# A one-core hybrid decoder step: VectorE takes the state-space block's products with C and its decay, and all sums of squares

## The chip, the cores and the metric

The kernel runs on one core of a Trainium2 chip. The metric is the device time of one execution in microseconds (us); lower is better. The engines named in the text are TensorE (PE, with its weight loads PEld), VectorE (DVE), ScalarE (ACT), GpSimd (POOL) and the DMA-issuing queue SP. Each engine works through its own instructions in the order in which they stand in the program.

## The reference

One layer over 1032 columns (1024 prompt positions and 8 sample positions), all in float32:

```
proj = rmsnorm(x) @ w_in                     # z | xBC | dt | v
xbc  = silu(causal_dwconv(xBC)); xs, B, C = split(xbc)
# state-space block, 24 heads of 64, chunks of 128 positions, state 64
acum = cumsum(dt * a)                        # within a chunk
mix  = (C B^T) * exp(acum_l - acum_s) * dt   # l >= s
y    = mix @ xs + (C * exp(acum)) @ h        # h: the state that enters the chunk
h    = exp(acum_last) * h + chunk_states     # the state that leaves it
y    = grouped_rmsnorm((y + d_skip * xs) * silu(z))
x    = x + [y | pooling(v)] @ w_out
u    = causal_dwconv(rmsnorm(x) @ w_up)
x    = x + (silu(gate(u)) * value(u)) @ w_down
out  = rmsnorm(x)
```

The states after the step are outputs too.

## The kernel before

Channels lie on partitions and positions along the free dimension. Every large product is made of three products of float32r parts: a weight tile is split into a high part (ACT, L140) and a low part (L141, on DVE or POOL; both stand in `weight_parts`), an activation tile likewise (L210, L211 in `split`), and the matmuls are L159 to L161, L1120 or L1307. The tile framework orders the instructions of each engine from a simulated timeline, so a change of an engine can move its neighbours; semaphores carry the waits.

**Input projection with the state-space block (`ssd_phase`).** Tiles of w_in go through PE one after another (`conv_tile`, `gate_tile`), three pieces of 344 columns each (24 matmuls a piece, 72 a tile). The three additions of the causal convolution are DVE's L516. Between the pieces stand the steps of the state-space block: two halves (q = 0 beside the convolution tiles, q = 1 beside the gate tiles), each with 8 chunks. Chunk c goes through

- `decay`: the exponent differences (DVE L538), 12 exponentials on ACT (L188, tile `mix`), and for c > 0 the tile `ce`: an exponential of 128x768 on ACT and its product with C (tile from `self.ctl`), L553 on POOL;
- `turn`: transposes on PE (L565, L571, L574), copies and products on DVE (L575, L576, L578 into `xd`, L583 into `mix`);
- `apply`: on PE the new chunk state (L597 into `pM`) and the output (L620 with `mix`, L630 with `ce` and the old state `h`, into `pY`). The state that goes on is h * decay (L606, POOL), to which DVE adds the chunk state (L610). DVE's L638 adds D times x.

`sample_tile` (L660 to L682) does one step for the 8 sample positions, all on POOL; tiles 0 to 2 come after half q = 0, tiles 3 to 6 inside half q = 1, each held behind the latest L606 (`self.pl`). `gate_tile` multiplies with silu(z) (L698, L700), and after three tiles `group_norm` squares on ACT (L712) and adds the squares up (L714, on POOL for the first two groups, on DVE for the others).

**End of w_out (`w_out_end`).** Two halves of 516 columns, 8 tiles n each. PE makes 24 matmuls of 258 columns a tile, DVE adds them to the residual x (L971), ACT squares the tile (L978), POOL adds the squares of n = 1 to 5 into `ssq` (L983); the last two squares and `ssq` go through a product with ones (L986, L997), which ACT turns into `rn` (L188). Beside the second half runs work on the first one (`beside`): scaling by `rn` in DVE's L1004 and splitting (L210, L211) into the operands of the up-projection.

**Up- and down-projection.** L1120 is fed by combined weights, made by DMAs that add (L1098 on SP loads, L1100 on POOL adds). The down-projection squares its output tiles on ACT (L1370, L1373) and adds the squares up on POOL (L1374).

Of the kernel before, what the change touches and what calls it, by code (L numbers as in the profile page):

```python
# [13 lines left out]
ALU = mybir.AluOpType  # L14
# [4 lines left out]
P = 128  # L19
# [26 lines left out]
TH, TQ = 516, 258  # L46
# [29 lines left out]
class Kernel:  # L76
    def __init__(self, ctx, tc, d):
        self.ctx, self.tc, self.nc, self.d = ctx, tc, tc.nc, d
        nc = self.nc
        pool = lambda name, bufs=1, **kw: ctx.enter_context(tc.tile_pool(name=name, bufs=bufs, **kw))  # L80
        self.const = pool("const")
        self.wpool = pool("weights")
        self.big = pool("big", 30)
        self.dram = pool("scratch", 1, space=DRAM)

        self.cst = self.const.tile([P, NCONST], F32, name="cst")
        self.mat = self.const.tile([P, NMAT], F32, name="mat")
        self.conv_st = self.const.tile([P, 16, 35], F32, name="conv_st")
        self.ones = self.const.tile([P, P], F32, name="ones")
        nc.vector.memset(self.ones, 1.0)  # L90
        self.zero = self.const.tile([P, P], mybir.dt.bfloat16, name="zero")
        nc.vector.memset(self.zero, 0.0)
        self.eps = self.const.tile([P, 1], F32, name="eps")
        nc.gpsimd.memset(self.eps, EPS)
        self.ident = self.mat[:, M_ID : M_ID + P]
        self.uid = 0
        self.lo_eng = nc.vector
        self.hooks = []
        self.pl = None
        self.tab = self.set = None  # L100
        self.table_set(EXPLN)

# [426 lines left out]
    def decay(self, q, c):  # L529

        nc = self.nc
        h0 = 12 * q
        mix = self.ph.tile([P, 12, P], F32, tag="mix", name=self.nm("mix"), bufs=2)
        src = lambda h, n, p: self.acd[c : c + 1, h * P : (h + n) * P].partition_broadcast(p)
        nc.sync.dma_start(mix.rearrange("p r l -> p (r l)"), src(h0, 12, P))
        hs = c * NH + h0

        nc.vector.scalar_tensor_tensor(  # L538
            out=mix, in0=self.acl[:, hs : hs + 12].unsqueeze(2).broadcast_to([P, 12, P]), scalar=80.0, in1=mix,
            op0=ALU.subtract, op1=ALU.max,  # L540
        )
        ce = None
        if c > 0:
            ce = self.ph.tile([P, 6, P], F32, tag="ce", name=self.nm("ce"), bufs=2)
            for g in range(2):
                rows = slice(64 * g, 64 * g + 64)
                nc.sync.dma_start(ce[rows].rearrange("p r l -> p (r l)"), src(h0 + 6 * g, 6, 64))
        for r in range(12):
            self.tables(mix[:, r], mix[:, r], AF.Exp, bias=self.acl[:, hs + r : hs + r + 1], scale=-1.0)
        if c > 0:  # L550
            self.tables(ce, ce, AF.Exp, scale=-1.0)
            cc = self.ctl[q][:, c * P : (c + 1) * P]
            nc.gpsimd.tensor_tensor(out=ce, in0=ce, in1=cc.unsqueeze(1).broadcast_to([P, 6, P]), op=ALU.mult)  # L553
        return mix, ce

    def turn(self, q, c, mix):
# [31 lines left out]
    def apply(self, q, c, mix, ce, xd, bT):  # L588

        nc = self.nc  # L590
# [11 lines left out]
        if c == 0:  # L602
            nc.scalar.activation(h1, pst[:, :384], AF.Copy)
        else:
            by_head = lambda t: t.rearrange("p (r x) -> p r x", x=64)
            self.pl = nc.gpsimd.tensor_tensor(  # L606
                out=by_head(h1), in0=by_head(h),
                in1=self.cd[:, c, q].unsqueeze(2).broadcast_to([P, 6, 64]), op=ALU.mult,
            ).ins
            nc.vector.tensor_tensor(out=h1, in0=h1, in1=pst[:, :384], op=ALU.add)  # L610
        self.hst[q] = h1
        if c == NCH - 1:
# [21 lines left out]
        for g in range(2):  # L634
            for i in range(3):
                k = 6 * q + 3 * g + i
                t = self.xs[k][:, cols]
# [69 lines left out]
    def group_norm(self, g):  # L707
        nc = self.nc
        sq = [self.short(SW, "sq") for _ in range(2)]
        nc.scalar.activation(sq[0], self.xs[3 * g], AF.Square)  # L710
        for i in range(1, 3):
            nc.scalar.activation(sq[1], self.xs[3 * g + i], AF.Square)  # L712
            eng = nc.gpsimd if g < 2 else nc.vector
            eng.tensor_tensor(out=sq[0], in0=sq[0], in1=sq[1], op=ALU.add)  # L714
        self.later(2, lambda: self.group_scale(g, sq))

    def group_scale(self, g, sq):
# [36 lines left out]
    def ssd_phase(self):  # L754
# [39 lines left out]
                queue.append(lambda c=c: step(c))  # L794

        def sample(i):
            with self.behind(self.pl):
                self.sample_tile(i // 6, i)

        self.lo_eng = nc.gpsimd  # L800
        for n in range(1, 6):
# [92 lines left out]
    def w_out(self, pf):  # L894
# [51 lines left out]
        def beside(n):  # L946
            if n == 0:
                return
            for k in {1: (0, 1), 2: (2, 3), 5: (4, 5), 6: (6, 7)}.get(n, ()):
                self.scale(k, 0)  # L950
            for k in {3: (0, 1), 4: (2, 3), 6: (4, 5), 7: (6, 7)}.get(n, ()):
                t = self.op_tile()
                self.split(self.x2[k][:, :TH], t[:, 0], t[:, 1])
                self.ops["p1" if k < half else "p2"].append((t[:, 0], t[:, 1]))
# [3 lines left out]
    def w_out_end(self, ops, t, beside=None):  # L958
# [5 lines left out]
        for n in range(KT):  # L964
# [13 lines left out]
                act = nc.scalar.activation(sq, x[:, cols], AF.Square).ins  # L978
            with self.behind(act):
                nc.scalar.dma_start(self.x2d[n][:, cols], x[:, cols])  # L980
            if n > 0:
                if n < 6:
                    nc.gpsimd.tensor_tensor(out=ssq, in0=ssq, in1=sq, op=ALU.add)  # L983
                else:
                    for q in range(2):
                        nc.tensor.matmul(  # L986
                            pb[q][:, :TQ], self.ones, sq[:, q * TQ : (q + 1) * TQ], start=(n == 6), stop=False
                        )
# [323 lines left out]
    def down(self, ops):  # L1312
# [49 lines left out]
        mksq = lambda: self.ph.tile([P, TH], F32, tag="sq", name=self.nm("sq"), bufs=2)  # L1362
        ssq = [self.bigt(F32, TOK, "ssq") for _ in range(2)]
        begun = set()

        def square(n, t):

            if t not in begun:
                begun.add(t)
                nc.scalar.activation(ssq[t][:, :TH], x2[n][:, half(t)], AF.Square)  # L1370
            else:
                sq = mksq()
                nc.scalar.activation(sq, x2[n][:, half(t)], AF.Square)  # L1373
                nc.gpsimd.tensor_tensor(out=ssq[t][:, :TH], in0=ssq[t][:, :TH], in1=sq, op=ALU.add)  # L1374

        def r_of(t):
            return ssq[t][:, TH : 2 * TH]
# [1 line left out]
        for p in DOWN[:-1]:  # L1379
# [17 lines left out]
            for m in range(NM):  # L1397
                ps = [self.gps() for _ in range(2)]
                for s in range(NS):
                    both = self.down_weights(p, m, s)  # L1400
                    for q in range(2):
                        self.piece(ps[q][:, :TQ], both, ops, s, q)
                for q in range(2):
                    sink(p, m, q, ps[q][:, :TQ])
                if p == "p6":
                    square(2 * m, 0)
                elif p == "p4":
                    square(2 * m + 1, 0)
                    square(2 * m + 1, 1)
        p = DOWN[-1]  # L1410
        ops = self.down_ops(p)
        both = {}
# [207 lines left out]
```

## Time and profile before

| | |
|---|---|
| median of 3 runs | 1403.05 us (1397.98, 1403.52, 1403.05) |
| the profiled execution's own time | 1399.9 us |
| its span, first to last instruction | 1398.1 us |
| mean granted TensorE clock | 0.984 |
| PE idle from 0 to 57 us, 142 to 238 us, 275 to 400 us, 682 to 735 us, 1160 us to the end | 4.0, 4.1, 11.9, 8.5, 9.9 us |

The stretch from 142 to 238 us holds half q = 0 of the state-space block, 275 to 400 us most of half q = 1, 682 to 735 us the end of w_out and the start of the up-projection, 735 to 1160 us the rest of the up-projection. The granted clock is the share of full speed that TensorE was given. In the rows of the profile, "out<-in" names tiles, and in brackets or after a bar stands how long the engine had been idle before and who ended that.

### The profile page before, as it was taken

To read this page: it belongs to the slowest core of one execution; us is meant where nothing else is said; L and a number is where in the kernel's file an instruction comes from. 1 tells how busy PE (TensorE), PEld (TensorE's weight loads), DVE (VectorE), ACT (ScalarE), POOL (GpSimd) and SP (SyncE) were. 2 spreads that over 40 slices of the span, in tenths; PEclk is the share of its full clock that TensorE was granted. 3 is DMA by queue.
4 is the path that set the end of the run, shared out by engine and by line. 5 is a ranking of instruction groups with operands and counts; after the bars stand their busy time and mean duration, and the time that the engine had idled before them with its cause. 6 is when DMAs were issued, how large, how long until landed. Compare 5 with 4: busy or idle time off the path is not lost.

```text
span 1398.1 us, 26823 instructions
## 1 busy us (share of the span) xinstructions
PE 1359.6 (97%) x10360; PEld 1312.8 (94%) x10360; DVE 986.9 (71%) x1501; ACT 701.3 (50%) x1408; POOL 496.8 (36%) x656
## 2 busy tenths in 40 slices
PE   8999999988999999999979999999999999999997
PEld 7799879977799999999979999999999999999997
DVE  6575899588864685755789867776776787567743
ACT  6346774655645451312447545554555465444451
POOL 4233466888578202122321222221222223214122
PEclk9999999999999999999989999999999999999999
DMA  7031235252331258665586877777777869657513
GB/s 250 1 109 39 87 121 173 81 162 98 95 105 63 73 187 280 224 199 187 151 199 151 210 202 197 199 191 200 176 179 199 204 214 324 225 180 238 179 54 121
DMA packets 117819, 228.08 MB, mean 163 GB/s; under 512 B 19884, under 2 KB 37116, under 8 KB 117692
## 3 DMA queue, kind: packets, MB, share of 16 engines
q1 hardware_dynamic: 73772, 130.21, 29.7%
q0 software_dynamic: 27056, 70.22, 20.0%
q10 hardware_dynamic: 16864, 25.95, 5.6%
q8 instruction: 81, 1.33, 0.4%
q14 instruction: 46, 0.38, 0.1%
HBM read 169.64 MB, written 45.15 MB: 154 GB/s over the span
## 4 chain that ended last, share of the span: by engine, by line
PE 82%; DVE 7%; DMA 3%; POOL 3%; issue 3%; ACT 2%; DVEq 0%; SPq 0%; POOLq 0%; ACTq 0%
PE g L1120 30%; PE g L1307 15%; PE g L160 10%; PE g L161 10%; PE g L159 10%; DVE wop L141 1%; DVE mix L583 1%; PE pY L620 1%; DVE xd L578 1%; POOL st L680 1%; DMA s<-wup 1%; DVE xs L516 1%; DVE xs L638 1%; PE pY L630 1%; DVE mix L538 1%
## 5 line engine op out<-in xcount | busy, mean ns | idle before, releaser
L1120 PE MATMUL g<-op,wop 128*128 128x258 f32 x3696 | 448.0, 284 | 3.9 <-ACT op L1045 3.7
L1120 PEld LDWEIGHTS g<-op,wop 128*128 128x128 f32 x3696 | 446.9, 190 | 4.7 <-ACT op L1045 4.1
L140 ACT ACTIVATE wop<-raw 128x512 fp32r<-128x512 f32 (+1 forms) x208 | 125.9, 608 | 228.1 <-PE g L161 134.3
L1307 PE MATMUL g<-op,wop 128*128 128x258 f32 x1848 | 224.9, 283 | 1.6 <-ACT op L210 0.8
L159 PE MATMUL g<-hh,wop 128*128 128x344 f32 x696 | 226.3, 325 | 0.0
L160 PE MATMUL g<-hl,wop 128*128 128x344 f32 x696 | 225.6, 324 | 0.0
L161 PE MATMUL g<-hh,wop 128*128 128x344 f32 x696 | 225.1, 323 | 0.0
L1307 PEld LDWEIGHTS g<-op,wop 128*128 128x128 f32 x1848 | 222.5, 189 | 2.6 <-ACT op L210 1.0
L141 DVE TENSOR_TENSOR wop<-raw,wop 128x512 fp32r<-128x512 f32 (+1 forms) x186 | 139.2, 752 | 88.6 <-ACT wop L140 86.6
L140 ACT ACTIVATE wop<-s 128x512 fp32r<-128x512 f32 (+1 forms) x136 | 83.6, 620 | 140.2 <-PE g L1307 51.9
L159 PEld LDWEIGHTS g<-hh,wop 128*128 128x128 f32 x696 | 132.5, 190 | 1.2 <-issue 1.1
L161 PEld LDWEIGHTS g<-hh,wop 128*128 128x128 f32 x696 | 132.3, 190 | 1.2 <-issue 1.2
L160 PEld LDWEIGHTS g<-hl,wop 128*128 128x128 f32 x696 | 132.2, 190 | 0.5 <-issue 0.4
L1100 POOL DMA_DIRECT2D s<-s x44 | 37.7, 857 | 249.8 <-DMA s<-wup 114.4
L1202 DVE SCALAR_TENSOR_TENSOR acc<-u,cst,acc 128x1048 f32<-128x1048 f32 x88 | 115.2, 1309 | 12.2 <-ACT acc L1200 10.6
L141 DVE TENSOR_TENSOR wop<-s,wop 128x512 fp32r<-128x512 f32 (+1 forms) x136 | 92.2, 683 | 36.3 <-ACT wop L140 33.9
L1180 DVE TENSOR_TENSOR u<-u,g 128x258 f32<-128x258 f32 (+2 forms) x176 | 58.2, 355 | 71.5 <-PE g L1120 64.1
L1177 ACT ACTIVATE u<-g 128x258 f32<-128x258 f32 (+2 forms) x220 | 69.6, 340 | 70.2 <-PE g L1120 70.0
L161 PE MATMUL g<-yh,wop 128*128 128x344 f32 x288 | 92.0, 319 | 0.0
L160 PE MATMUL g<-yl,wop 128*128 128x344 f32 x288 | 91.9, 320 | 0.0
L159 PE MATMUL g<-yh,wop 128*128 128x344 f32 x288 | 91.8, 319 | 0.0
L1277 POOL DMA_DIRECT2D g<-td x77 | 41.1, 539 | 122.9 <-DVE op L211 69.4
(276 smaller groups left out, 2279.8 us busy)
## 6 DMA issues: line engine op xcount, KB each, us to landing
s<-wup SPq DMA_DIRECT2D x88, 256.0 KB, 3.1
g<-td POOLq DMA_DIRECT2D x77, 258.0 KB, 4.6
raw<-wup SPq DMA_DIRECT2D x66, 256.0 KB, 3.9
raw<-win SPq DMA_DIRECT2D x58, 256.0 KB, 2.6
mix<-acd SPq DMA_DIRECT2D x16, 768.0 KB, 4.5
td<-acc ACTq DMA_DIRECT2D x22, 516.0 KB, 6.2
s<-wup POOLq DMA_DIRECT2D x44, 256.0 KB, 5.4
s<-s POOLq DMA_DIRECT2D x44, 256.0 KB, 3.7
```

The costliest lines, as they stand in the source:

```text
L140: self.nc.scalar.activation(hi, raw[:, :w], AF.Copy)
L141: lo_eng.tensor_tensor(out=lo, in0=raw[:, :w], in1=hi.bitcast(F32), op=ALU.subtract)
L159: nc.tensor.matmul(ps[:, :n], wh, xh[:, sl], start=(first and k == 0), stop=False)
L160: nc.tensor.matmul(ps[:, :n], wh, xl[:, sl], start=False, stop=False)
L161: nc.tensor.matmul(ps[:, :n], wl, xh[:, sl], start=False, stop=(final and k == last))
L1100: nc.gpsimd.dma_start(t, raw[acc] if acc in raw else w[acc][j], accum_op=ALU.add)
L1120: nc.tensor.matmul(out, a, b, start=(p in OPENS and j == 1), stop=(j == 12), skip_group_check=True)
L1177: a = nc.scalar.activation(out, ps[:, s], AF.Copy, scale=-1.0 if p in ("p5", "p4") else 1.0)
L1180: nc.vector.tensor_tensor(out=out, in0=out, in1=ps[:, s], op=op)
L1202: nc.vector.scalar_tensor_tensor(out=acc, in0=u[:, k : k + FW], scalar=self.c("fw", 3 * n + k), in1=acc, op0=ALU.mult, op1=ALU.add)
L1277: self.loaded = self.nc.gpsimd.dma_start(st[:, j], self.td[i + j][ROW[p]]).ins
L1307: self.pe = nc.tensor.matmul(out, a, b, start=(s == 0 and i == 0 and j == 0), stop=(s == len(PIECES) - 1 and i == nk - 1 and j == 2),).ins
```

## The change

Four places lose their POOL instruction and gain the same one on DVE: the product of `ce` with C, the decay of the state, the squares of the first two norm groups, and the squares at the end of w_out and of the down-projection. The last two are now added one tile late: `w_out_end` adds the square of tile n - 1 behind the last addition of tile n, and the down-projection empties a list `waiting` at its next square. `sample_tile` is no longer held behind the decay. In `beside`, the scaling of tiles 6 and 7 and the splitting of tiles 4 and 5 move from n = 6 to n = 7, behind the last addition of w_out.

```
 decay():
-            nc.gpsimd.tensor_tensor(out=ce, in0=ce, in1=cc...broadcast_to([P, 6, P]), op=ALU.mult)
+            nc.vector.tensor_tensor(out=ce, in0=ce, in1=cc...broadcast_to([P, 6, P]), op=ALU.mult)
 apply():
-            self.pl = nc.gpsimd.tensor_tensor(
+            nc.vector.tensor_tensor(
                 out=by_head(h1), in0=by_head(h),
                 in1=self.cd[:, c, q].unsqueeze(2).broadcast_to([P, 6, 64]), op=ALU.mult,
-            ).ins
+            )
 group_norm():
-            eng = nc.gpsimd if g < 2 else nc.vector
-            eng.tensor_tensor(out=sq[0], in0=sq[0], in1=sq[1], op=ALU.add)
+            nc.vector.tensor_tensor(out=sq[0], in0=sq[0], in1=sq[1], op=ALU.add)
 ssd_phase():
-            with self.behind(self.pl):
-                self.sample_tile(i // 6, i)
+            self.sample_tile(i // 6, i)
 w_out():
-            for k in {1: (0, 1), 2: (2, 3), 5: (4, 5), 6: (6, 7)}.get(n, ()):
+            for k in {1: (0, 1), 2: (2, 3), 5: (4, 5), 7: (6, 7)}.get(n, ()):
                 self.scale(k, 0)
-            for k in {3: (0, 1), 4: (2, 3), 6: (4, 5), 7: (6, 7)}.get(n, ()):
+            for k in {3: (0, 1), 4: (2, 3), 7: (4, 5, 6, 7)}.get(n, ()):
 w_out_end():
+            if 1 < n < 7:
+                with self.behind(add):
+                    nc.vector.tensor_tensor(out=ssq, in0=ssq, in1=before, op=ALU.add)
             if n > 0:
-                if n < 6:
-                    nc.gpsimd.tensor_tensor(out=ssq, in0=ssq, in1=sq, op=ALU.add)
-                else:
+                before = sq
+                if n >= 6:
 down():
+        def add_up():
+            while waiting:
+                t, sq = waiting.pop(0)
+                nc.vector.tensor_tensor(out=ssq[t][:, :TH], in0=ssq[t][:, :TH], in1=sq, op=ALU.add)
         def square(n, t):
+            add_up()
...
-                nc.gpsimd.tensor_tensor(out=ssq[t][:, :TH], in0=ssq[t][:, :TH], in1=sq, op=ALU.add)
+                waiting.append((t, sq))
```

The order on the engines moves with it. First place: POOL at the start of half q = 1, before. `st`, `stt` and `xs` belong to sample tile 3, `ce` and `h` to chunk 1 of the state-space block.

```order
L666 DMA st_2999<-st_ssm 128x512
L672 TENSOR_TENSOR st_2999<-st_2999,dA 128x512
L553 TENSOR_TENSOR ce_2843<-ce_2843,xs_1561 128x768
L673 TENSOR_TENSOR stt_3002<-st_2999,stt_3002 128x512
L606 TENSOR_TENSOR h_3048<-h_2932,cd 128x384
L674 DMA ssm_s<-stt_3002 128x512
```

The same two products now stand on DVE (line numbers of the changed file: L552 is the product with C, L605 the decay, L582 and L577 the products of `turn`, L637 the output's additions). The first of them:

```order
L582 TENSOR_TENSOR mix_2775<-mix_2775,cb_2818 128x768
L637 SCALAR_TENSOR_TENSOR xs_1824<-xs_1824,cst,pY_2927 128x128
L637 SCALAR_TENSOR_TENSOR xs_2087<-xs_2087,cst,pY_2927 128x128
L637 SCALAR_TENSOR_TENSOR xs_2330<-xs_2330,cst,pY_2927 128x128
L552 TENSOR_TENSOR ce_2843<-ce_2843,xs_1561 128x768
```

`ce_2843` stood behind a load and a product of the sample tile; it now stands behind products and additions of chunk 0, and the decay `h_3048` follows a dozen rows later between the products of chunk 1.

Second place: DVE at the end of half q = 0, where the last chunk's output is added (L638 into `xs_723` and the five after it), before:

```order
L516 SCALAR_TENSOR_TENSOR xs_2330<-u_2103,cst,xs_2330 128x1056 x2
L610 TENSOR_TENSOR h_2382<-h_2382,pM_2379 128x384
L516 SCALAR_TENSOR_TENSOR xs_2330<-u_2103,cst,xs_2330 128x1056
L638 SCALAR_TENSOR_TENSOR xs_723<-xs_723,cst,pY_2377 128x128
L638 SCALAR_TENSOR_TENSOR xs_832<-xs_832,cst,pY_2377 128x128
```

and now, where L515 is the convolution's addition and L609 the addition to the state:

```order
L605 TENSOR_TENSOR h_2382<-h_2247,cd 128x384
L515 SCALAR_TENSOR_TENSOR xs_2330<-u_2103,cst,xs_2330 128x1056
L537 SCALAR_TENSOR_TENSOR mix_2775<-acl,mix_2775 128x1536
L140 TENSOR_TENSOR wop_2621<-raw_2619,wop_2621 128x512
L609 TENSOR_TENSOR h_2382<-h_2382,pM_2379 128x384
L140 TENSOR_TENSOR wop_2626<-raw_2624,wop_2626 128x512
L515 SCALAR_TENSOR_TENSOR xs_2330<-u_2103,cst,xs_2330 128x1056
L515 SCALAR_TENSOR_TENSOR xs_2469<-u_2346,cst,xs_2469 128x1056
L637 SCALAR_TENSOR_TENSOR xs_723<-xs_723,cst,pY_2377 128x128
```

The last chunk's output now comes inside the next convolution tile (`xs_2469`); on PE its L620 stand 58 matmuls of the projection later than before.

Third place: DVE at the last tile of w_out, from the addition to tile 6 (`x_5322`) to that of tile 7 (`x_5324`), before:

```order
L971 TENSOR_TENSOR x_5322<-x_5322,g_7280 128x258
L1004 SCALAR_TENSOR_TENSOR x_5322<-x_5322,cst,rn_7014 128x516
L1004 SCALAR_TENSOR_TENSOR x_5324<-x_5324,cst,rn_7014 128x516
L211 TENSOR_TENSOR op_7301<-x_5318,op_7301 128x516
L211 TENSOR_TENSOR op_7304<-x_5320,op_7304 128x516
L141 TENSOR_TENSOR wop_7469<-raw_7399,wop_7469 128x512
L971 TENSOR_TENSOR x_5324<-x_5324,g_7312 128x258
```

and now (L968 adds to the residual, L981 adds a square, L210 splits, L140 splits a weight):

```order
L968 TENSOR_TENSOR x_5322<-x_5322,g_7279 128x258
L981 TENSOR_TENSOR ssq_7020<-ssq_7020,sq_7254 128x516
L140 TENSOR_TENSOR wop_7469<-raw_7399,wop_7469 128x512
L968 TENSOR_TENSOR x_5324<-x_5324,g_7304 128x258
L968 TENSOR_TENSOR x_5324<-x_5324,g_7318 128x258
L1004 SCALAR_TENSOR_TENSOR x_5322<-x_5322,cst,rn_7014 128x516
L1004 SCALAR_TENSOR_TENSOR x_5324<-x_5324,cst,rn_7014 128x516
L210 TENSOR_TENSOR op_7339<-x_5318,op_7339 128x516
```

Between the two additions stood two scalings, two splits and a weight; now a square and a weight. On SP, the seven loads `s<-wup` (L1098) now stand ahead of the load `raw_7869`, behind which they stood.

More of the change, by code (lines that the diff above doesn't have):

```diff
@@ L552, in decay @@
             cc = self.ctl[q][:, c * P : (c + 1) * P]
-            nc.gpsimd.tensor_tensor(out=ce, in0=ce, in1=cc.unsqueeze(1).broadcast_to([P, 6, P]), op=ALU.mult)
+            nc.vector.tensor_tensor(out=ce, in0=ce, in1=cc.unsqueeze(1).broadcast_to([P, 6, P]), op=ALU.mult)
         return mix, ce
@@ L1364, in down @@
         begun = set()
+        waiting = []
+        def add_up():
+            while waiting:
+                t, sq = waiting.pop(0)
+                nc.vector.tensor_tensor(out=ssq[t][:, :TH], in0=ssq[t][:, :TH], in1=sq, op=ALU.add)
         def square(n, t):
+            add_up()
             if t not in begun:
```

2 lines of the change are left out of this document (1 added, 1 removed).

## The prediction, made blind

> **What bounds the kernel now.** I read the page's busy times first, then the busy times of each engine in stretches, then the timeline at the slices where TensorE stands idle, then the durations of the operations that move.
>
> ```profile
> PE 1359.6 (97%) x10360; PEld 1312.8 (94%) x10360; DVE 986.9 (71%) x1501; ACT 701.3 (50%) x1408; POOL 496.8 (36%) x656
> ```
>
> PE is busy for 97% of the span and the change removes no matmul from it, so only idle and slow PE time can be won. Where that lies is told by the stretches (length, then busy time of PE, PEld, DVE, ACT and POOL, granted clock, DMA):
>
> ```profile
> 142.00:238.00 96.00, 91.88 (x809) 80.35 (x808) 90.58 (x130) 64.41 (x140) 57.06 (x45) 0.98 0.42 133
> 155.00:165.00 10.00, 8.09 (x66) 7.35 (x63) 9.93 (x17) 6.12 (x15) 3.75 (x5) 0.83 0.55 170
> 240.00:275.00 35.00, 35.00 (x226) 34.64 (x225) 20.83 (x19) 17.88 (x39) 29.46 (x36) 1.00 0.24 80
> 275.00:400.00 125.00, 113.15 (x884) 97.57 (x883) 98.79 (x142) 73.85 (x154) 92.36 (x96) 0.92 0.38 116
> 640.00:682.00 42.00, 42.00 (x321) 41.65 (x320) 21.38 (x41) 14.48 (x25) 8.65 (x9) 1.00 0.55 167
> 682.00:735.00 53.00, 44.53 (x319) 42.52 (x319) 47.57 (x76) 27.21 (x58) 15.88 (x14) 0.90 0.68 172
> 1160.00:1398.10 238.10, 228.16 (x1878) 226.11 (x1876) 147.36 (x265) 109.92 (x209) 60.79 (x95) 0.99 0.55 183
> ```
>
> Half q = 0 (142 to 238) loses 4.1 us to idle PE and about 0.02 x 96 = 1.9 us to a lower clock: 6.0. Half q = 1 (275 to 400) loses 11.9 and 0.08 x 125 = 10.0: 21.9. The end of w_out (682 to 735) loses 8.5 and 0.10 x 53 = 5.3: 13.8. These 41.7 us are all that the change can reach; in the first two stretches DVE is the fullest engine beside PE.
>
> Three places show what PE waits for (start, duration, idle before):
>
> ```profile
> 288.63 1.42 POOL L672 TENSOR_TENSOR st<-st,dA 128x512 f32<-128x512 f32 x1 [3.15 <-DMA st<-st_ssm]
> 290.01 1.80 POOL L553 TENSOR_TENSOR ce<-ce,xs 128x768 f32<-128x768 f32 x1
> 325.31 2.48 POOL L714 TENSOR_TENSOR sq<-sq,sq 128x1056 f32<-128x1056 f32 x1
> 325.37 5.26 DVE L141 TENSOR_TENSOR wop<-raw,wop 128x512 fp32r<-128x512 f32 x1
> 371.35 4.74 DVE L578 TENSOR_TENSOR xd<-xd,wd 128x768 f32<-128x768 f32 x1
> 372.78 1.81 POOL L553 TENSOR_TENSOR ce<-ce,xs 128x768 f32<-128x768 f32 x1
> ```
>
> At 288 us the product of `ce` stands in POOL's queue behind a sample tile that waits 3.15 us for its load. At 325 and 371 us DVE products of two SBUF tensors take 5.26 and 4.74 us while POOL runs its own: the two engines slow each other. How much, the spread of each line says (min/median/max in ns):
>
> ```profile
> L583 DVE TENSOR_TENSOR mix<-mix,cb x32: 944/958/2792, 138.4 to 387.2; 128x768 f32<-128x768 f32 x32
> L516 DVE SCALAR_TENSOR_TENSOR xs<-u,cst,xs x48: 1300/1318/2875, 81.3 to 266.0; 128x1056 f32<-128x1056 f32 x48
> L141 DVE TENSOR_TENSOR wop<-raw,wop x186: 547/686/5256, 228.1 to 1342.0; 128x512 fp32r<-128x512 f32 x142, 128x384 fp32r<-128x384 f32 x44
> L714 POOL TENSOR_TENSOR sq<-sq,sq x4: 2437/2486/2502, 325.3 to 391.9; 128x1056 f32<-128x1056 f32 x4
> L714 DVE TENSOR_TENSOR sq<-sq,sq x4: 1258/1619/2042, 421.2 to 469.5; 128x1056 f32<-128x1056 f32 x4
> ```
>
> against the groups of q = 0 (142 to 238 us) and q = 1 (275 to 400 us), busy time and mean:
>
> ```profile
> L516 DVE SCALAR_TENSOR_TENSOR xs<-u,cst,xs 128x1056 f32<-128x1056 f32 x15 | 26.1, 1741 | 0.1
> L583 DVE TENSOR_TENSOR mix<-mix,cb 128x768 f32<-128x768 f32 x14 | 16.0, 1144 | 0.8 <-ACT mix L188 0.8
> L578 DVE TENSOR_TENSOR xd<-xd,wd 128x768 f32<-128x768 f32 x7 | 9.5, 1354 | 0.0
> L553 POOL TENSOR_TENSOR ce<-ce,xs 128x768 f32<-128x768 f32 x7 | 18.5, 2641 | 24.2 <-ACT ce L188 24.1
> L606 POOL TENSOR_TENSOR h<-h,cd 128x384 f32<-128x384 f32 x7 | 10.2, 1459 | 11.2 <-DVE h L610 7.6 <-PE pY L630 3.6
> ...
> L583 DVE TENSOR_TENSOR mix<-mix,cb 128x768 f32<-128x768 f32 x15 | 21.6, 1442 | 0.0
> L141 DVE TENSOR_TENSOR wop<-raw,wop 128x512 fp32r<-128x512 f32 x12 | 16.1, 1347 | 2.2 <-ACT wop L140 2.2
> L578 DVE TENSOR_TENSOR xd<-xd,wd 128x768 f32<-128x768 f32 x8 | 13.7, 1708 | 0.0
> L553 POOL TENSOR_TENSOR ce<-ce,xs 128x768 f32<-128x768 f32 x7 | 13.8, 1968 | 10.3 <-ACT ce L188 10.3
> L606 POOL TENSOR_TENSOR h<-h,cd 128x384 f32<-128x384 f32 x7 | 7.8, 1112 | 5.8 <-DVE cb L576 3.8 <-PE pY L630 1.9
> ```
>
> Above its median DVE pays in q = 0: 15 x 0.42 (L516) + 14 x 0.19 (L583) + 7 x 0.40 (L578, same size as L583) = 11.8 us; in q = 1: 15 x 0.48 + 12 x 0.66 + 8 x 0.75 = 21.1 us. This is the price of the work that POOL does beside it.
>
> **The change, part by part.** *Half q = 0.* DVE gains 7 products of 128x768 at 0.96 us and 7 of 128x384; the trace has none of these on DVE with a decay broadcast, so the bounds are half of L583's 0.96 and all of it, and I take 0.55, near the half, since the size is half: 7 x (0.96 + 0.55) = 10.6 us. POOL loses 18.5 + 10.2 = 28.7 of its 57.1 us, half; if DVE's surcharge falls likewise, it loses 5.9 of 11.8 (bounds 0 and 11.8). DVE then needs 90.6 + 10.6 - 5.9 = 95.3 us. It ran 90.6 of 96 us, 94%; at that share 95.3 us take 101. The order gives room: the last chunk's matmuls stand 58 projection matmuls later, at 35.0/226 = 0.155 us each 9 us of cover, in a stretch (240 to 275) where DVE idles 14 of 35 us. So PE need not wait longer than now, and the wait for `ce` behind other POOL work is gone: of the 6.0 us lost I take 3 back (bounds: -5, if the cover does not hold, and +6).
>
> At this place stands a rule on the clock. Between 155 and 165 us PE idled at most 1.9 us, and the granted clock of these 10 us was 0.83, that is 1.7 us lost. The Trainium skill ("TensorE: Matmul & The Clock Gate", section on the HAM clock gate) has the clock halved after an idle window of about 3.4 us; by it so short a gap costs no clock, the lower clock of this stretch could not be won back, and the upper bound would be the idle 4.1 us instead of 6.0. The row speaks against it: the drop follows a gap shorter than that.
>
> *Half q = 1.* The same 10.6 us come to DVE, and four sums of squares at L714's DVE median of 1.62: 6.5 us. POOL loses 13.8 + 7.8 + 9.9 (4 x 2.486) = 31.5 of 92.4 us, 34%, which lifts 7.2 of DVE's 21.1 us. DVE: 98.8 + 10.6 + 6.5 - 7.2 = 108.7; at 94% that is 115.6 us, so of the 125 us at most 9.4 can go before DVE is the bound. What goes first: the stall at 288 us (the product no longer stands behind a load), and the parts of those at 325 and 371 us that the removed POOL rows made. Late next is the DVE product itself, behind up to six additions of its own chunk. The sample tiles lose their hold and get POOL to themselves; L700, which needs their result on DVE, cannot come later for that. I take 8 (bounds 0 and 21.9).
>
> *End of w_out.* The rows (the x2 are pairs):
>
> ```profile
> 682.61 0.42 DVE L971 TENSOR_TENSOR x<-x,g 128x258 f32<-128x258 f32 x1 [1.02 <-PE g L161]
> 684.28 1.80 DVE L141 TENSOR_TENSOR wop<-raw,wop 128x512 fp32r<-128x512 f32 x1
> 701.29 1.41 DVE L1004 SCALAR_TENSOR_TENSOR x<-x,cst,rn 128x516 f32<-128x516 f32 x2
> 702.62 1.29 DVE L211 TENSOR_TENSOR op<-x,op 128x516 fp32r<-128x516 f32 x2
> 704.44 0.74 DVE L971 TENSOR_TENSOR x<-x,g 128x258 f32<-128x258 f32 x2
> 705.96 1.14 PE L986 MATMUL pM<-sq,ones 128*128 128x258 f32 x2 [2.68 <-ACT sq L978]
> 707.40 3.37 SPq L1098 DMA_DIRECT2D s<-wup  x7
> 724.53 6.73 PE L1120 MATMUL g<-op,wop 128*128 128x258 f32 x34 [3.38 <-ACT op L1045]
> ```
>
> From 682.6 to the last addition at 705.2 DVE is full (47.6 of 53 us in the stretch) and PE waits for it. Five L141 cost 1.80 beside POOL's squares instead of 0.69: -5.6 us. Five squares at 1.29/2 come in: +3.2. The pair of scalings and one pair of splits leave: -1.41 - 1.29 = -2.7. DVE's path is 5.1 us shorter. PE's own pace limits it: 42.0 us for 321 matmuls is 0.131, six tiles of 24 take 18.8 us, from 682.6 to 701.4 against 705.2, so 3.8 us; the stretch holds wider matmuls too, so it may be a little more. The moved 2.7 us fall into the time in which DVE waits for `rn`, so they cost nothing; if `rn` came at once, they would cost 2.7. The loads `s<-wup` no longer stand behind `raw_7869`, but still behind ACT's copies for the next tile, so the wait of 3.38 us at 724.5 shrinks little. I take 4 (bounds 1, with the moved 2.7 us uncovered, and 5.1 + 3.4 = 8.5).
>
> *First half of w_out, down-projection.* From 640 to 682 us PE has no idle time: 0. In the down-projection DVE gains ten additions of about 0.65, 6.5 us, of the 91 us that it idles after 1160; each comes one tile late, so ACT's square has long been there: 0, bounds -1 and +1.
>
> Sum: 3 + 8 + 4 = 15 us off 1399.9 gives 1384.9. The profiled execution lies 3.2 below the median of the runs and 1.6 below their mean (1401.5); 15 off the mean is 1386.5. I forecast 1386.
>
> **Rivals.** *DVE takes the place of POOL as the bound, so that both halves keep their length.* For it: 94% busy in q = 0, and 17 us new work per half q = 1. Against it: the surcharges of 4.74 and 5.26 us for 0.7 to 0.96 us of work. Only w_out's 4 us are left: 1397.5.
>
> *The end of w_out gives nothing* because the weights' chain behind `s<-wup`, not DVE, sets when the up-projection runs on. For it: 3.38 us at 724.5. Against it: PE's wait for the last square at 706. Then 1401.5 - 11 = 1390.5.
>
> *Slower: DVE's queue now waits for ACT.* POOL waited for the exponential of `ce`:
>
> ```profile
> POOL ce L553 <- ACT ce L188: 34.3, 7, 10.3
> ```
>
> On POOL 34.3 us cost little; on DVE everything behind waits too. If two thirds, 23 us, came to lie on DVE's path, the 15 us would turn into a loss of 8: 1409.5. It decides from 22 us on. Against it: in the new order the product stands behind L583, whose exponentials ACT makes just before, and behind up to six additions. The same page of the Trainium skill (section on the array's architecture) calls ACT and DVE strict first-in first-out queues; by that rule this rival's mechanism holds, and no run here shows its size yet.
>
> **Chances.** The forecast (1377 to 1394) 0.64; DVE the bound 0.17; w_out without gain 0.11; slower 0.08. A change within 0.5% (7 us, 1396 to 1410) can hardly be told from none. Faster: 0.64 + 0.11 + a little of the second, 0.78; same 0.14; slower 0.08. The range, 1371 to 1399, takes in the first three and, below, the larger bounds of q = 1 and w_out; the likeliest alone is 1377 to 1394.
>
> **What would show it.** Right: L141 and L578 without 4 us maxima in q = 1, the PE stall near 290 us gone, L141 at 0.69 beside w_out, the last L971 about 4 us earlier after the first half's end, granted clock over 0.95 from 275 to 400 us. Wrong: DVE rows waiting on ACT `ce`, PE waits on L583 or L610 that were not there, or the same surcharges beside the sample tiles alone.

## The result, and the profile after

| | before | after |
|---|---|---|
| median of the runs | 1402.34 us (1397.98 to 1403.52, 4 runs) | 1379.03 us (1377.45 to 1383.41, 4 runs) |
| profiled execution, its span | 1399.9, 1398.1 | 1383.41, 1381.6 |
| granted clock, mean | 0.984 | 0.992 |

The ratio is 0.9853 (95% interval 0.9817 to 0.989): 23.3 us between the medians, 16.5 between the two profiled executions. The forecast was 1386, or 1384.9 for the profiled execution. Why the two differences are not the same is taken up below, with a second profile of the changed kernel.

The page's busy times first, then the same stretches as before (length, then busy time of PE, PEld, DVE, ACT and POOL, granted clock, DMA):

```profile
PE 1350.8 (98%) x10360; PEld 1303.9 (94%) x10360; DVE 1000.4 (72%) x1553; ACT 700.1 (51%) x1408; POOL 432.9 (31%) x604
```

```profile
142.00:238.00 96.00, 95.12 (x838) 83.52 (x836) 90.65 (x142) 66.62 (x144) 28.57 (x24) 1.00 0.37 120
155.00:165.00 10.00, 9.12 (x80) 8.60 (x80) 9.96 (x18) 4.82 (x12) 1.71 (x4) 1.00 0.59 169
275.00:400.00 125.00, 118.17 (x919) 103.23 (x916) 114.36 (x165) 77.19 (x153) 87.01 (x88) 0.96 0.41 127
310.00:315.00 5.00, 2.54 (x36) 2.01 (x25) 5.00 (x10) 4.44 (x14) 4.76 (x5) 1.00 0.09 23
315.00:320.00 5.00, 5.00 (x24) 5.00 (x23) 5.00 (x11) 4.80 (x5) 1.60 (x6) 0.66 1.02 343
682.00:735.00 53.00, 46.37 (x348) 44.73 (x347) 49.89 (x91) 31.70 (x72) 10.38 (x12) 0.94 0.73 182
```

Half q = 0 lost 4.1 us of PE time and now loses 0.9, at full clock. In half q = 1 PE is busy 118.2 instead of 113.2 of 125 us although DVE's busy time rose from 98.8 to 114.4: DVE is fuller than before and PE still does more, so DVE's total load was not what held PE there. What PE waits for between 275 and 400 us (in total, times, longest), before and then after:

```profile
PE pY L630 <- POOL ce L553: 5.8, 2, 4.7
PE pM L597 <- DVE xd L578: 3.2, 1, 3.2
PE pT L571 <- DVE cb L576: 2.8, 1, 2.8
```

```profile
PE pM L564 <- DVE h L609: 2.6, 2, 2.5
PE pY L619 <- DVE mix L582: 2.2, 3, 1.6
PE pM L596 <- DVE xd L577: 1.7, 2, 1.6
```

The 5.8 us behind POOL are gone (they were 9.2 us in the second profile of the old recurrence, that of the other part alone). What PE waits for DVE stays about the same: 6.0 us before (4.9 in that second profile), 6.7 after, with a wait of 0.2 us that is not shown. The minimum, median and maximum of the lines that paid for POOL's neighbourhood (ns):

```profile
L582 DVE TENSOR_TENSOR mix<-mix,cb x32: 936/946/2041, 138.1 to 372.6; 128x768 f32<-128x768 f32 x32
L577 DVE TENSOR_TENSOR xd<-xd,wd x16: 941/948/2333, 138.9 to 371.8; 128x768 f32<-128x768 f32 x16
L140 DVE TENSOR_TENSOR wop<-raw,wop x186: 546/684/2295, 218.6 to 1325.5; 128x512 fp32r<-128x512 f32 x142, 128x384 fp32r<-128x384 f32 x44
L515 DVE SCALAR_TENSOR_TENSOR xs<-u,cst,xs x48: 1298/1310/2671, 81.0 to 262.2; 128x1056 f32<-128x1056 f32 x48
```

The maxima of 4.74 and 5.26 us are gone, those near 2 us are not. From the DVE groups of q = 1 (busy time and mean; what ended the idle time), the lines that moved:

```profile
L140 DVE TENSOR_TENSOR wop<-raw,wop 128x512 fp32r<-128x512 f32 x14 | 13.6, 998 | 0.0
L577 DVE TENSOR_TENSOR xd<-xd,wd 128x768 f32<-128x768 f32 x7 | 9.7, 1392 | 0.0
L552 DVE TENSOR_TENSOR ce<-ce,xs 128x768 f32<-128x768 f32 x7 | 7.2, 1031 | 2.0 <-ACT ce L187 2.0
L712 DVE TENSOR_TENSOR sq<-sq,sq 128x1056 f32<-128x1056 f32 x4 | 6.6, 1659 | 0.7 <-ACT sq L711 0.7
L605 DVE TENSOR_TENSOR h<-h,cd 128x384 f32<-128x384 f32 x7 | 4.9, 694 | 0.0
```

The end of w_out (timeline rows: start, duration, idle before):

```profile
688.85 0.68 DVE L140 TENSOR_TENSOR wop<-raw,wop 128x512 fp32r<-128x512 f32 x1
689.45 0.74 DVE L968 TENSOR_TENSOR x<-x,g 128x258 f32<-128x258 f32 x2
690.12 1.41 DVE L1004 SCALAR_TENSOR_TENSOR x<-x,cst,rn 128x516 f32<-128x516 f32 x2
690.98 0.70 PE L986 MATMUL pM<-sq,ones 128*128 128x258 f32 x2 [0.48 <-ACT sq L975]
693.02 3.27 SPq L1098 DMA_DIRECT2D s<-wup  x7
708.74 0.63 ACT L139 ACTIVATE wop<-s 128x512 fp32r<-128x512 f32 x1 [4.48 <-DMA s<-s]
709.27 0.62 ACT L1045 ACTIVATE op<-x 128x516 fp32r<-128x516 f32 x1
709.94 6.57 PE L1120 MATMUL g<-op,wop 128*128 128x258 f32 x34 [5.46 <-ACT op L1045]
```

L140 costs 0.68, PE waits 0.48 instead of 2.68 us for the last square, and the moved scalings, which use the first half's `rn`, run at 690.12, while the second half's is not there yet. But the wait of 3.38 us at 724.5 has become 5.46. PE starts right behind an ACT copy of an operand, which ends near 709.9; that copy stands on ACT behind the copy of a weight at 708.74, and this one waited 4.48 us for the sum `s<-s`.

For all runs below, three times of TensorE: the start of w_out (first matmul on `yh`, the high part of the state-space block's output), from the first matmul on `ph` (the high part of the pooled operands) to the first of the up-projection (the end of w_out), and from there to the first of the down-projection; then the median of the run's executions.

| kernel | w_out starts | end of w_out | up-projection | median |
|---|---|---|---|---|
| before | 513.7 | 58.0 | 448.5 | 1402.3; 1399.5 to 1400.6 beside the runs below |
| after | 503.4 | 51.9 | 449.0 | 1379.0 |
| after, second profile | 505.4 | 51.9 | 449.4 | 1383.2 |
| recurrence's part alone | 500.6 | 58.1 | 445.8 | 1384.5 |
| the other part alone | 514.9 | 51.7 | 450.1 | 1395.7 |
| without the moved pairs | 499.2 | 55.0 | 446.6 | 1381.7 |
| h back on POOL | 509.2 | 51.7 | 450.3 | 1391.7 |
| ce back on POOL | 516.9 | 51.7 | 451.4 | 1399.4 |
| sums back on POOL | 523.4 | 51.9 | 450.2 | 1403.2 |
| scratch products in q = 0 | 514.4 | 51.9 | 449.4 | 1394.5 (one run) |
| scratch additions, w_out | 501.5 | 56.2 | 449.8 | 1386.6 (one run) |
| scratch copies, w_out | 497.8 | 53.5 | 448.9 | 1379.4 (one run) |
| late products held | 507.7 | 51.9 | 447.5 | 1379.1 |
| the same, 22 `fst` buffers | 496.8 | 51.9 | 448.1 | 1379.3 |

Eight of these run the changed recurrence undisturbed, with the same instructions in the same order on DVE, ACT and SP, and start w_out anywhere from 496.8 to 507.7 us, 501.6 in the mean. The three latest (503.4, 505.4, 507.7) are those with a granted clock of 0.96 or 0.97 between 275 and 400 us; the other five had 0.99 or 1.00. Which of the two brings the other is not shown. So a single profile says nothing about less than some 5 us in q = 1, while the end of w_out repeats within 0.2 us and the up-projection within 3.

### The profile page after: what moved, and what is told of

The parts are those of the page before. It is cut to its first block, busy times and chain, and to the rows that moved or that the text cites. A ratio compares the mean times of both kernels' runs of the same rounds, so it can differ in the third digit from the quotient of the medians.

```text
span 1381.6 us, 26777 instructions
## 1 busy us (share of the span) xinstructions
PE 1350.8 (98%) x10360; PEld 1303.9 (94%) x10360; DVE 1000.4 (72%) x1553; ACT 700.1 (51%) x1408; POOL 432.9 (31%) x604
## 5 line engine op out<-in xcount | busy, mean ns | idle before, releaser
L140 DVE TENSOR_TENSOR wop<-raw,wop 128x512 fp32r<-128x512 f32 (+1 forms) x186 | 129.0, 698 | 70.7 <-ACT wop L139 68.9
L140 DVE TENSOR_TENSOR wop<-s,wop 128x512 fp32r<-128x512 f32 (+1 forms) x136 | 90.9, 673 | 36.9 <-ACT wop L139 34.8
```

Source lines behind the costliest of these rows:

```text
L140: lo_eng.tensor_tensor(out=lo, in0=raw[:, :w], in1=hi.bitcast(F32), op=ALU.subtract)
```

## Experiments

**The two parts by themselves.** The recurrence's part: the diff without its changes in `w_out`, `w_out_end` and `down`.

> Only the recurrence's part of the change: ce's product, h's decay and the sums of squares of the gated groups on DVE, the sample tiles without their hold; the end of w_out and the down-projection as before. Theory (POOL's two-operand work slows DVE beside it, and ce stood behind POOL's other work; the gains of the places add up): w_out starts 10 us earlier than before (3.5 of it by the end of q = 0), the end of w_out is as before (L141 beside the squares 1.80 us), the whole 10 us below before, ratio 0.993. Rival (the places hang together, what is won early is partly lost again at w_out's end by work that stands on the same queue): less than 6 us below before. Rival (DVE the new bound): no gain, 1.000.

1384.54 us, ratio 0.988 (0.9848 to 0.9912); w_out starts 13.1 us earlier than before, its end is unchanged at 58.1. That is more than the theory's 10, and nothing is lost later: the first rival falls, and so does the second. The other part:

> Only the other part: the sums of squares of w_out's end and of the down-projection on DVE one tile late, and the scalings and splits of the last two pairs behind the last addition; the recurrence as before. Theory: L141 beside w_out's second half at 0.69 us, the last addition about 5.5 us earlier, the whole 6 us below before, ratio 0.996; the start of w_out as before. Rival (the chain of the loads s<-wup sets the end): the last addition earlier, but the wait for the first weights that are sums longer by as much, ratio 1.000.

1395.66 us, ratio 0.9975 (0.9954 to 0.9997). The end of w_out is 6.3 us shorter, as the theory has it, the up-projection 1.6 longer (its first wait for late weights is 5.73 us, 3.38 before): the rival is right for a quarter of the gain. (1.6 us is less than the 3 by which this stage varies; that PE's wait grew by 2.4 us is what speaks for it.) 4.7 us remain in these two columns, 4.0 between the medians. Both parts together, 15.2 + 4.0 us off 1399.7, make 1380.5, near the whole change.

**The moved pairs.**

```
-            for k in {1: (0, 1), 2: (2, 3), 5: (4, 5), 7: (6, 7)}.get(n, ()):
+            for k in {1: (0, 1), 2: (2, 3), 5: (4, 5), 6: (6, 7)}.get(n, ()):
...
-            for k in {3: (0, 1), 4: (2, 3), 7: (4, 5, 6, 7)}.get(n, ()):
+            for k in {3: (0, 1), 4: (2, 3), 6: (4, 5), 7: (6, 7)}.get(n, ()):
```

> The whole change without its moved pairs: the scalings of x2 6 and 7 and the splits of 4 and 5 stand again behind the sixth addition of w_out's second half, as before; all else as after. Theory (the moved 2.7 us of DVE work now fall into the wait for rn and cost nothing there): the last addition of w_out 2.0 to 2.7 us later than in the changed kernel, the whole 2 us above it, ratio to before about 0.987. Rival (PE's pace of 3.1 us a tile and the loads s<-wup set the end): same as the changed kernel, within 0.5 us at the first matmul of the sixth product.

The last addition comes 2.5 us later against the first `ph` matmul (51.6 instead of 49.0), as the theory has it. But the whole lies between theory and rival: the end of w_out is 3.1 us longer and the up-projection 2.4 shorter, so 0.7 us remains of moving the pairs. PE's first three waits there are 2.42, 0.52 and 0.24 us, against 5.46, 0.32 and 0.37 with the pairs moved: most of what is won in front of the chain of loads is waited for behind it, which is the rival's mechanism. The medians, 1381.7 with 0.9866 (0.9834 to 0.9897), cannot tell so little.

**h back on POOL, with the hold of the sample tiles** (`nc.vector` to `nc.gpsimd` at the decay, and `with self.behind(self.pl)` around the sample tile).

> The whole change with h's decay back on POOL and the sample tiles held behind it again; ce's product stays on DVE. Theory (the gain goes with the POOL time taken away; h was 18.0 of 60.2 us): a third of the 10 us of the recurrence is lost, the whole 3 us above the changed kernel, ratio to before 0.988. Rival (ce's place in POOL's queue was all of it): same as the changed kernel. Rival (h on DVE lengthens the DVE path of the chunk, POOL was the better place): 1 to 3 us below the changed kernel.

1391.71 us, ratio 0.9944 (0.9923 to 0.9966): 8.6 us above the higher and 12.7 above the lower median of the changed kernel, not 3. None of the three theories has that. PE's waits between 275 and 400 us and the rows behind the longest (POOL, then PE):

```profile
PE pM L565 <- DVE h L610: 8.9, 2, 8.6
```

```profile
294.66 1.03 POOL L672 TENSOR_TENSOR st<-st,dA 128x512 f32<-128x512 f32 x1 [3.02 <-DMA st<-st_ssm]
295.77 1.26 POOL L673 TENSOR_TENSOR stt<-st,stt 128x512 f32<-128x512 f32 x1
297.33 0.60 POOL L674 DMA_DIRECT2D ssm_s<-stt  x1 [0.30 <-POOL stt L673]
297.95 1.27 POOL L675 TENSOR_TENSOR st<-stt,bc 128x512 f32<-128x512 f32 x1
299.16 0.83 POOL L606 TENSOR_TENSOR h<-h,cd 128x384 f32<-128x384 f32 x1
...
300.64 0.47 PE L565 MATMUL pM<-mat,xs 128*128 128x128 f32 x1 [8.62 <-DVE h L610]
```

The decay takes 0.83 us and stands behind a sample tile's load and four of its instructions. The addition on DVE that needs it holds PSUM's only `pM` bank, and PE's next transpose waits for that bank.

**ce back on POOL** (`nc.vector` to `nc.gpsimd` at the product; no hold).

> The whole change with ce's product back on POOL; h's decay stays on DVE and the sample tiles stay without their hold. Theory, as the run with h back on POOL has changed it (of the recurrence's 13 us two thirds are the queue: whatever of the chunk stays on POOL gets caught behind a sample tile that waits for its load): TensorE waits for ce at least once for 4 to 9 us between 275 and 400 us, the start of w_out comes 6 to 9 us later than in the changed kernel, the whole 7 to 9 us above it. Rival (the gain goes with the POOL time taken away, ce 32.3 of 60.2 us): 5 us above, lost in both halves alike. Rival (h alone was the place that counted): same as the changed kernel.

1399.42 us, ratio 1.0002 (0.9979 to 1.0025): the whole gain is gone. What PE waits for, and the rows at the longest wait:

```profile
PE pY L629 <- POOL ce L552: 13.4, 2, 9.7
```

```profile
291.53 1.04 POOL L671 TENSOR_TENSOR st<-st,dA 128x512 f32<-128x512 f32 x1 [1.82 <-DMA st<-st_ssm]
292.53 1.80 POOL L552 TENSOR_TENSOR ce<-ce,xs 128x768 f32<-128x768 f32 x1
...
294.38 1.54 PE L629 MATMUL pY<-ce,h 64*64 64x128 f32 x12 [9.65 <-POOL ce L552]
```

The mechanism is the theory's (one wait of 4 to 9 us), the size is twice as large, and the rival with shares in POOL's busy time falls.

**The sums of squares back on POOL** (L712 for the first two groups; no hold).

> The whole change without its four sums of squares of the gated groups: those of the first two groups are on POOL again. TensorE does not wait for them, so this changes contention alone: POOL gets 9.9 us more between 300 and 400 us, DVE loses 6.5 us. Theory of the queue (what counts between 275 and 400 us is that ce and h are off POOL): the start of w_out within the 497.8 to 503.4 us of the runs so far, at most 2 us above their mean of 500.5. Rival (contention counts here too): 4 us or more above, 504.5 and later. Rival (DVE, 91% busy there, is the bound, and loses work): 497 or earlier.

1403.22 us, ratio 1.0013 (0.9986 to 1.004). I had written that TensorE does not wait for these sums. It does, over ScalarE. PE's longest wait, then ACT's, then rows of POOL, ACT and PE:

```profile
PE g L158 <- ACT z L692: 18.8, 1, 18.8
```

```profile
ACT sq L711 <- POOL sq L713: 24.8, 1, 24.8
```

```profile
322.00 1.18 POOL L671 TENSOR_TENSOR st<-st,dA 128x512 f32<-128x512 f32 x1 [5.38 <-DMA st<-st_ssm]
...
347.28 2.42 POOL L713 TENSOR_TENSOR sq<-sq,sq 128x1056 f32<-128x1056 f32 x1
349.73 1.08 ACT L711 ACTIVATE sq<-xs 128x1056 f32<-128x1056 f32 x1 [24.80 <-POOL sq L713]
350.72 0.79 ACT L692 ACTIVATE z<-g 128x344 f32<-128x344 f32 x2
351.21 0.65 PE L158 MATMUL g<-hh,wop 128*128 128x344 f32 x1 [18.79 <-ACT z L692]
```

From 322 to 347 us POOL works through sample tiles; the addition of 2.4 us stands behind them. ACT's next square needs the buffer that the addition reads, the copies of `z` stand behind that square on ACT, and PE finds no free bank. Between 325 and 350 us ACT is busy for 0.27 of 25 us. The Trainium skill ("TensorE: Matmul & The Clock Gate", section on the array's architecture) calls ACT's queue a strict first-in first-out queue; these rows agree, 24.8 us long. So each of the three operations, alone on POOL, costs most of the recurrence's gain or more than all of it. They are no shares of a sum. Nor are they the price that the kernel before paid: it has all three on POOL and begins w_out at 513.7 us, earlier than the last two runs (516.9 and 523.4), and it has the hold of the sample tiles, which these two lack.

**POOL's load without anyone who needs its result.** In q = 0, behind each `ce`:

```
+            if q == 0:
+                dum = self.ph.tile([P, 512], F32, tag="st", ...)
+                flat = ce.rearrange("p r l -> p (r l)")
+                for _ in range(3):
+                    nc.gpsimd.tensor_tensor(out=dum, in0=flat[:, :512], in1=flat[:, 256:], op=ALU.mult)
```

> The whole change, and in the half q = 0 three products of 128x512 on POOL behind each ce, into a scratch tile that nothing reads: the changed kernel's DVE work with about the POOL load of before, and no one who waits for POOL. Theory (there are no sample tiles in q = 0; the 4 us won there by the last L515 at 262 instead of 266 us are DVE's lower surcharge): the last L515 3 to 4 us later, near 266 us, its mean between 142 and 238 us back from 1.50 to about 1.74 us. Rival (ce and h came late from POOL, contention plays no part): last L515 within 0.7 us of 262.2.

The last L515 starts at 275.3 instead of 262.2 us, 13 later, three times the theory's amount, at a mean of 1.58 us between 142 and 238 us, where 1.74 was expected. The theory's sign holds, its size does not, and the run is not clean: POOL's queue also makes the lower parts of weights there (mean 2.22 us instead of 1.92), and loads of `ce` waited 9.0 us for the scratch products. It shows that POOL work whose result nobody needs can cost DVE and PE this much, by slower rows and by buffers that come free late together, not how the 4 us of q = 0 divide. L577's size at that place says what DVE paid (L582 in this file):

```profile
L582 DVE TENSOR_TENSOR xd<-xd,wd 128x768 f32<-128x768 f32 x7 | 9.9, 1416 | 0.0
```

It is 0.945 us in the changed kernel and 1.354 before.

In w_out's second half, for tiles 2 to 6, an addition or a copy into scratch (L968's place is unchanged, L1009 is L1004 of the changed file):

```
...
+            if t == 1 and 1 < n < 7:
+                nc.gpsimd.tensor_tensor(out=dum, in0=dum, in1=sq, op=ALU.add)   # or: nc.gpsimd.tensor_copy(dum, sq)
```

> The whole change, and in w_out's second half on POOL an addition of each square to a scratch tile (128x516, two operands) for tiles 2 to 6, as POOL made it before; nothing reads the scratch. Theory (DVE and POOL slow each other): L140 beside it again near 1.8 us instead of 0.68, the stretch from the first matmul of the pooled operands to the first of the up-projection 51.9 us back to 55 to 58. Rival (the shorter DVE queue and the moved pairs made the gain, not the neighbour): L140 near 0.7, the stretch 52.

> As the run with additions on POOL, but POOL copies each square into the scratch tile (one operand). Theory, if the price hangs on two operands from SBUF on both engines: L140 at 0.7 to 0.8 us beside the copies, the stretch 52 us. Rival (any POOL work of that length beside DVE slows it): L140 near 1.8 us, the stretch 55 to 58 us.

The stretch grows from 51.9 to 56.2 with the additions, as the theory said, but the payer is another: L140 stays at 0.68, and the scalings and splits pay. DVE groups between 664 and 706 us, each time with the POOL group that they meet (the additions' run, then the copies'):

```profile
L1009 DVE SCALAR_TENSOR_TENSOR x<-x,cst,rn 128x516 f32<-128x516 f32 x13 | 11.8, 938 | 0.2 <-ACT rn L187 0.2
L210 DVE TENSOR_TENSOR op<-x,op 128x516 fp32r<-128x516 f32 x8 | 7.4, 958 | 0.0
L986 POOL TENSOR_TENSOR dum<-dum,sq 128x516 f32<-128x516 f32 x5 | 7.7, 1546 | 50.9 <-ACT sq L975 50.9
```

```profile
L1009 DVE SCALAR_TENSOR_TENSOR x<-x,cst,rn 128x516 f32<-128x516 f32 x16 | 12.3, 793 | 0.2 <-ACT rn L187 0.2
L210 DVE TENSOR_TENSOR op<-x,op 128x516 fp32r<-128x516 f32 x8 | 6.0, 787 | 0.0
L986 POOL COPY dum<-sq 128x516 f32<-128x516 f32 x5 | 4.4, 882 | 50.8 <-ACT sq L975 50.8
```

Against 747 and 684 in the changed kernel, DVE pays 13 x 0.191 + 8 x 0.274 = 4.7 us for the additions, and the stretch is 4.3 longer; for the copies 16 x 0.046 + 8 x 0.103 = 1.6, and 1.6 longer. So my split by the number of operands falls, since a copy slows DVE too; but the rival's 55 to 58 us does not come either: a copy is shorter, and costs less for each us that it takes (1.6 of 4.4 us against 4.7 of 7.7). One meeting in the copies' run (DVE, then POOL) shows how:

```profile
670.66 1.78 DVE L1009 SCALAR_TENSOR_TENSOR x<-x,cst,rn 128x516 f32<-128x516 f32 x2
670.93 0.95 POOL L986 COPY dum<-sq 128x516 f32<-128x516 f32 x1 [40.12 <-ACT sq L975]
```

The pair of scalings takes 1.42 alone. The second would begin near 671.4, and ends at 672.44, 0.56 us after the copy's end at 671.88: it did most of its 0.75 us after the copy. The Trainium skill ("SBUF — State Buffer", section "Who interferes with whom") says that a DVE instruction with two SBUF inputs contends with a POOL instruction that reads SBUF, and calls the ports that the two share an exclusive lock. These rows agree but for 0.2 us, which may lie in POOL's recorded span.

**The wait at the start of the up-projection.** On PE two matmuls of p6 stand ahead of 48 of the early products; here all late matmuls are held behind the last early one. A second run besides gives `fst`, the tile of a small load on SP ahead of `s<-wup`, 22 buffers instead of 4.

```
...
+        early = self.pe
         for j in js:
-            self.blocks(self.up_weights(j, LATE, raws[j]), ops, pairs[j][2], LATE, ps[j])
+            self.blocks(self.up_weights(j, LATE, raws[j]), ops, pairs[j][2], LATE, ps[j], early)
```

The changed kernel ran beside both, since so small a difference needs the same chip.

> The changed kernel once more, on the same chip and beside the same runs of before as the three others of this call. What each theory expects: the five runs so far with this recurrence began w_out at 497.8 to 503.4 us, the profiled run of the result is the latest of them; so the start of w_out at 500.5 (497 to 504), the whole about 1381, ratio 0.986. A start of w_out at 503 again, and 1383, would say that the result's profile was a usual one.

> The changed kernel, and in the up-projection the matmuls of the late products (p5, p6, ...) of the first three pairs are held behind the last early one (p1, p2), so that the 48 early matmuls which now follow two of p6 come first. Theory (TensorE idles 5.46 us before 709.94 because two p6 matmuls stand ahead of the last two early blocks and wait for weights that come by the chain of loads s<-wup, s<-s; 48 matmuls at 0.123 us are 5.9 us of cover): the wait gone or under 1 us, the first matmul of the down-projection 4.5 to 5.5 us earlier after the first of the up-projection (444 instead of 449), the whole 5 us below the changed kernel. Rival (the chain is only met later, by p5 or p7 of the first pair, whose weights come by the same chain): less than 1.5 us.

> As the run with the held late products, and besides with 22 buffers instead of 4 for fst, so that the loads s<-wup of the first pairs no longer stand on SyncE's queue behind a small load that waits for ScalarE's copies. Theory (with the cover in place TensorE no longer waits for this chain): the same as with the hold alone within 1 us. Rival (the chain is still late for the next products): the loads s<-wup start 2 to 3 us earlier against the last L997 and another 1 to 3 us go.

The second profile of the changed kernel began w_out at 505.4, later than expected. Its six runs go from 1378.38 to 1385.95, so 23.3 us between the first medians flattered the change a little: 17.4 us lie between the medians of these later runs (1400.59 and 1383.15), with ratio 0.9861 (0.983 to 0.9892). Holding the late products takes PE's first waits of the up-projection from 5.55, 0.33 and 0.37 to 2.73, 1.74 and 0.30 us, 1.5 less, and the stage from 449.4 to 447.5. With the buffers the loads `s<-wup` start 2.8 us earlier against the last L997, as the second rival has it, but no more is won (448.1). So the gain is near the first rival's size, not the theory's; but the cover is there, and with the hold alone PE waits for DVE and not for the chain:

```profile
711.50 5.50 PE L1121 MATMUL g<-op,wop 128*128 128x258 f32 x24 [2.73 <-DVE u L1182]
718.74 5.72 PE L1121 MATMUL g<-op,wop 128*128 128x258 f32 x46 [1.74 <-DVE u L1182]
```

Between 705 and 712 us DVE is busy for 7.00 of 7 us. The medians are 1379.1 (0.9844, 0.9813 to 0.9876) and 1379.3 (0.9834, 0.9803 to 0.9865), 4 us below the changed kernel beside them, of which the stage shows 1.3 to 1.9; the rest is within the spread of q = 1. It is at best a small further gain.

## Why the prediction was right, step by step

- *Half q = 0, +3.* The last L515 begins 3.8 us earlier (266.0 to 262.2; 261.8 to 263.6 in the undisturbed runs). Of DVE's surcharge 15 x 0.239 + 14 x 0.084 + 7 x 0.409 = 7.6 us went, where 5.9 were taken, and L552 and L605 cost 0.948 and 0.545 there, where 0.96 and 0.55 were taken. The clock came back with it: 0.83 between 155 and 165 us became 1.00. By the rule of a 3.4 us window (the Trainium skill, "TensorE: Matmul & The Clock Gate", section on the HAM clock gate) that could not be won back. The row after speaks against it as the row before did: at 310 us PE idles 2.46 us, and the next 5 us run at 0.66. A gap of this length does not always cost clock: the same one stands in nine profiles, and in two of them (the recurrence's part alone and 22 `fst` buffers) the clock from 310 to 325 us is 1.00, against 0.89 in the other seven.
- *Half q = 1, +8.* In the profiled execution 6.5 us; over eight profiles of the changed recurrence and two of the old (513.7 and 514.9) both halves together bring 12.8, some 9 of them here. The total fits, the weights of its reasons do not. The 8 was taken between wide bounds (0 and 21.9) and not added up from the three stalls, so that it fits is in part luck. The one cap that I had worked out, 9.4 us, came from DVE's load, which did rise to 114.4 where I had 108.7, and did not matter. What the waits above show is that PE no longer waits behind sample tiles in POOL's queue (5.8 or 9.2 us to none), the stall at 288 us, which I had as one item of three; the granted clock rose with it from 0.92 to 0.96. The stalls near 325 and 371 us are gone too, but PE's waits for DVE are 6.7 us in sum as against 6.0. Two of them, for L609 (2.6 us) and L582 (2.2 us), are waits that the profile before has not, which I had listed as a sign of being wrong; they are too small to turn the result, and the second profile of the old recurrence has 3.4 us at the latter line as well. That any one of the three operations, put on POOL without the others, brings most of the gain back or more was in none of my steps. Nor was the value of the four sums: I counted them as 6.5 us of DVE work against POOL relief.
- *End of w_out, +4.* The last addition comes 4.6 us earlier after the first `ph` matmul, the up-projection starts 6.1 earlier, and its own stage is 0.5 longer than before, 1.6 in the part alone, 3.2 against the recurrence's part alone. So 3 to 5.6 us are left. The moved pairs cost nothing, as I had it, and shorten DVE's path by 2.5 us where I counted 2.7; but next to nothing of it is left behind the chain of loads. That wait, which was to shrink a little, grew from 3.38 to 5.46 us: this step was wrong, and the 4 fits because the up-projection starts 6.1 us earlier, more than the 3.8 that I took from PE's pace. The rival that the chain `s<-wup` gives all back had the mechanism, but not the size.
- *First half of w_out, down-projection, 0.* 137.4 us from the first `yh` to the first `ph` matmul in both; from the first to the last matmul of the down-projection 230.5 and 229.9 us.
- *The sum, 1386.* The first median lies 7 us below it, the second 3. The gain was forecast too small by either; how much of this is the spread of q = 1 cannot be told.
- *DVE as the bound.* No: 91% busy with PE faster. But what PE still waits for there is all DVE's. *DVE waits for ACT's exponential.* That wait exists, once, for 2.0 us, a tenth of what it needed.

Not tried: the sums or `ce` on POOL with the hold of the sample tiles kept. With the hold, h cost 8.6 to 12.7 us; without it, the others 16 to 24 between the medians. How much of that is the missing hold and how much the operation stays open, and so does how the recurrence's gain divides between POOL's queue and the two engines' slowing each other.

## What to carry to other kernels

An operation that TensorE needs, directly or over another engine's queue, does not belong in the queue of an engine that runs long, patient work with loads in it: here an operation of 0.8 to 2.4 us cost TensorE 9 to 19 us of waiting. Price a move by what stands ahead of it in the queue, not by busy shares; a fuller engine can be the faster one. And follow a gain into the next stage: part of the 6 us won in front of the up-projection was waited for again behind its chain of loads.

## What the runs showed of the hardware that I had not expected

- A POOL copy of one operand slows DVE as well (0.36 us of DVE per us of copy, 1.6 of 4.4; 0.61 for additions, 4.7 of 7.7).
- Who pays is a matter of meeting: the same POOL additions took 1.1 us from each L141 before and nothing from L140 now, but 0.19 and 0.27 us a piece from the scalings and splits.
- An idle time of 2.5 us on TensorE was followed by 5 us at a granted clock of 0.66; in two of nine profiles the same gap cost no clock.
- Executions of the same recurrence, with the same order on DVE and ACT, differ by up to 11 us at one place: the start of w_out, 496.8 to 507.7 us.
- A late DMA on ScalarE's queue can hold TensorE by way of another instruction: the copy of a weight waited 4.48 us for a sum, and the copy of the operand behind it released TensorE after 5.46 us.
